# Encoder layer on one core: y stores of the late local blocks behind the next place's matmul, the last strip's 272-token block first, one y load of the third pass a tile sooner

## The chip, the cores and the metric

The kernel runs on one core of a Trainium2 chip. A core has five engines that each run their own list of instructions in order: PE (TensorE, matmuls), DVE (VectorE), ACT (ScalarE), POOL (GpSimd) and SP (SyncE, which here issues the transfers). An instruction waits on semaphores that other engines or transfers raise. The metric is the device time of one execution in microseconds, the median of three runs.

## The reference

One layer of an encoder is applied to two groups of tokens, a prompt of 1024 and a sample of 256, with the same 16 meta tokens put in front of each. Cut to what matters:

```python
def encoder_layer(h, ...):                       # h: (B, N, 2048), N = 16 + 1024 or 16 + 256
    u = rms_norm(h, norm_w) @ w_in               # 2048 x 6656: qa, ka, va, za, qb, kb, vb, zb
    qa, ka = rope(rms_norm(qa)), rope(rms_norm(ka))
    ya = global_gqa(qa, ka, va) * silu(za)       # 8 heads on 2 key heads, all keys
    qb, kb = rms_norm(qb), rms_norm(kb)
    yb = neighbourhood_attention(qb, kb, vb, rpb) * silu(zb)   # 8 heads, a window of 8 x 16 tokens and the meta keys
    return h + concatenate([ya, yb]) @ w_out     # 2048 x 2048
```

The outputs are the prompt's and the sample's tokens without the meta tokens, in float32. A head is 128 wide, so w_in is 52 strips of 128 columns.

## The kernel before

Every float32 product is three matmuls: the operands are split into a high part (cast on ACT, L62) and a low part (subtracted on DVE, L63), and hi·hi, hi·lo and lo·hi are added in PSUM.

**Projection.** Tokens are projected in two chunks. Chunk 1 has 512 tokens (sample, 240 of the prompt, meta). Chunk 2 has the other 784 of the prompt as two blocks of 512 and 272 (`BL`), whose split activations lie in the tiles "xa"/"x" and "xb". `strips` (L177 to L216) projects one strip: four chunks `c` of four k-tiles; in each chunk it loads w_in (`wr`, L194, from SP), splits it to `wh` and `wl`, and runs block by block four k-tiles of three matmuls (L211 to L213). The two blocks have a PSUM bank each (`pp`, four banks in all). After the second and the fourth chunk, `run_due` gives one "place" to attention work that is due.

**Evacuation.** A q strip goes through `qk_evac`: square on ACT (`ms`, L226), sum over partitions on POOL (`m`, L228), reciprocal square root on ACT and DVE (`rs_l`, `rs_r`, L72 to L74), product with the bank (L245), and a store to DRAM (`q2d`, L248). A z strip goes through `z_evac`: `z` (L267) reads the bank, four ACT functions, `za` (L272), `zt` (L275), and a store (`zd`, L785). Both go over the 512 block and then the 272 block. `z` of L267 is the last reader of a z strip's bank.

**Attention.** Global heads run between strips at some 750 to 1300 us. Then 24 late strips give 48 places, in which local heads 0 to 6 run: `scores` (L447, L280, L281 on PE) in one place, `values` (a y block of 256 tokens, L323 to L328) two places later. A y block is stored to `yd` (L328, from SP) as soon as it is there. The last strip of all is head 7's z. Head 7's keys and query are loaded back by `load_kq`: `qfull` (L801, L802) reads `q2d`, ACT (L62) and DVE (L63) split it to `q`. Head 7 runs in the first pass of the output projection.

**Output projection.** `outproj` makes seven passes (1, 2, 5, 6, 7, 3, 4) over five token tiles and two column halves; one step is 24 matmuls into a bank `pq` (L969 to L971). The `pq` pool takes over the four banks of `pp`. Its weights `ww` (L946 or L944) are loaded into the slots that xb leaves and split to `wm` in the slots of xa; the y operands are `yl`/`yh` in passes 1 and 2 (L910) and sums of two 512 KB loads `yr` (L904, `ysum` L930) from the third pass on.

**Order.** The Python code is traced, and a scheduler sets each engine's list when the kernel is built. It keeps the dependencies, goes by priority else, and `issue_after(x)` holds what is traced inside behind `x`. From the second pass on the lists keep the order of the code (`in_order`). A tile of a pool with one buffer can be written again only when its last reader, a transfer too, is done.

Of the kernel before, what the change touches and what calls it, by code (L numbers as in the profile page):

```python
# [12 lines left out]
F32 = mybir.dt.float32  # L13
# [7 lines left out]
P = 128  # L21
# [3 lines left out]
M3 = 3 * NMETA  # L25
# [14 lines left out]
QB = 256  # L40
# [8 lines left out]
NT = TH // P  # L49
# [6 lines left out]
class Kern:  # L56
# [120 lines left out]
    def strips(self, jobs, getx):  # L177


        nc, tc = self.nc, self.tc  # L180
        out = [[pool.tile([P, 512], F32, tag=tag, name="pp") for pool, tag in pools] for _, _, pools in jobs]
        for c in range(KT // WCH):
            ws = []
            for s, _, _ in jobs:
                with tc.high_priority(offset=self.woff):
                    w = self.raw.tile([P, WCH, P], F32, tag="raw", name="wr")
                    single = self.projected == 2 and c == 0 and not self.second
                    for i in range(0, WCH, 1 if single else WCH):
                        e = i + (1 if single else WCH)
                        self.lastw = nc.sync.dma_start(w[:, i:e], self.io["w_in"][s][:, c * WCH + i:c * WCH + e, :]).ins  # L190
                    wh = self.w.tile([P, WCH, P], F32R, tag="wh", name="wh")
                    wl = self.w.tile([P, WCH, P], F32R, tag="wl", name="wl")
                    if self.second and s not in AGAIN:
                        nc.sync.dma_start(wl[:].bitcast(F32), self.wld[s][:, c * WCH:(c + 1) * WCH, :])  # L194
                        nc.scalar.copy(wh[:], w[:])
                    else:
                        for i in range(0, WCH, 1 if single else WCH):
                            e = i + (1 if single else WCH)
                            self.lastsplit = self.split(wh[:, i:e], wl[:, i:e], w[:, i:e])
                            self.lasthi = self.hi  # L200
                ws.append((wh, wl))
                if not self.second and s not in AGAIN:
                    nc.sync.dma_start(self.wld[s][:, c * WCH:(c + 1) * WCH, :], wl[:].bitcast(F32))
            for b in range(len(jobs[0][1])):
                for k in range(WCH):
                    kt = c * WCH + k
                    xh, xl = getx(kt)[b]
                    first, last = kt == 0, kt == KT - 1
                    for (wh, wl), ps, (_, blocks, _) in zip(ws, out, jobs):
                        p, n = ps[b], blocks[b][1]  # L210
                        nc.tensor.matmul(p[:, :n], wh[:, k, :], xh[:, :n], start=first, stop=False)  # L211
                        nc.tensor.matmul(p[:, :n], wh[:, k, :], xl[:, :n], start=False, stop=False)  # L212
                        self.lastmm = nc.tensor.matmul(p[:, :n], wl[:, k, :], xh[:, :n], start=False, stop=last).ins  # L213
            if c % 2:
                self.run_due()
        return out  # L216

    def run_due(self):
        for _, f, a in next(self.due, ()):
            with self.tc.issue_after(self.lastmm):  # L220
                f(*a)
# [55 lines left out]
    def meta_scores(self, pm, meta, qh, ql, scale):  # L277

        nc = self.nc
        nc.tensor.matmul(pm[:ML + M3], meta, qh, start=True, stop=False)  # L280
        nc.tensor.matmul(pm[:ML + M3], meta, ql, start=False, stop=True)  # L281
        sm, sl = (self.sm.tile([M3, QB], F32, tag=n, name=n) for n in ("Sm", "Sl"))
        nc.scalar.activation(sl[:], pm[ML:ML + M3], AF.Copy, scale=scale)
        nc.vector.scalar_tensor_tensor(out=sm[:], in0=pm[:M3], scalar=scale, in1=sl[:], op0=ALU.mult, op1=ALU.add)
        return sm
# [27 lines left out]
    def put_y(self, po, tot, zs, ydst):  # L313

        nc = self.nc
        r = self.t.tile([P, QB], F32, tag="t", name="r")
        nc.scalar.activation(r[:], tot[:], AF.Ln)
        nc.scalar.activation(r[:], r[:], AF.Exp, scale=-1.0)
        nc.vector.tensor_tensor(out=tot[:], in0=tot[:], in1=r[:], op=ALU.mult)
        nc.vector.scalar_tensor_tensor(out=r[:], in0=tot[:], scalar=2.0, in1=r[:], op0=ALU.subtract, op1=ALU.mult)  # L320
        y = self.y.tile([P, QB], F32, tag="y", name="y")
        if len(zs.shape) == 3:
            nc.vector.tensor_tensor(out=y[:].rearrange("p (g r) -> p g r", g=4), in0=po[:].rearrange("p (g r) -> p g r", g=4),  # L323
                                    in1=zs, op=ALU.mult)
        else:
            nc.vector.tensor_tensor(out=y[:], in0=po[:], in1=zs, op=ALU.mult)
        nc.vector.scalar_tensor_tensor(out=y[:], in0=y[:], scalar=-1.0, in1=r[:], op0=ALU.mult, op1=ALU.mult)
        nc.sync.dma_start(ydst, y[:].rearrange("p (g r) -> p g r", g=ydst.shape[1]))  # L328

    def attend(self, q, zs, keys, meta, vals, vmeta, ydst):  # L330

# [243 lines left out]

    def chunk1(self):
        nc, io = self.nc, self.io
        self.due = iter(())
        self.woff, self.second, self.projected, self.sums = 0, False, 0, self.w_sums()
        self.scale2 = [self.one2.tile([P, T2], F32, tag=n, name=n) for n in ("rb2", "eb2")]  # L580
        self.xsq = {}
# [91 lines left out]
        for g in range(2):  # L673
# [4 lines left out]
            else:  # L678
                k, = pr(k_strip(KA + g, g, kw, True))
                (v, vm), = pr(v_strip(VA + g, g))  # L680
            for h in range(4 * g, 4 * g + 4):
                z, = pr(z_strip(ZA + h, h))
                q, = pr(q_strip(QA + h, h, qw, True))
                run(h, q, z, k, v, vm, None)
        for h in range(8):
            kj, qj = kb_strip(KB + h, 2 + h, kwb), qb_strip(QB_ + h, 8 + h, qwb)
            k, = pr(kj)
            q, = pr(qj)
            vj, zj = v_strip(VB + h, 2 + h), z_strip(ZB + h, 8 + h)
            if h < 7:  # L690
                (v, vm), = pr(vj)
                z, = pr(zj)
# [5 lines left out]
    def chunk2(self):  # L698
        nc, io = self.nc, self.io
# [26 lines left out]
        def v_rows_of(s, g):  # L726

            def evac(ps):
                for p, (o, n) in zip(ps, BL):
                    self.rows_out(self.v_rows(p, o, n), n, self.vn[g], C1P + o)  # L730
            return s, BL, evac
# [104 lines left out]

        def values(h, b):
            next(blocks.pop((h, b)), None)

        def local_heads():  # L840
            places = [[] for _ in range(LATE)]
# [18 lines left out]
        late = []  # L860
# [4 lines left out]
        def fill(n):  # L865
            for _ in range(min(n, len(late))):
                pr(late.pop(0))

        for g in range(2):
            if g == 0:  # L870
                k, _ = pr(k_strip(KA, 0, kw, True), v_rows_of(VA, 0))
            else:
                k, = pr(k_strip(KA + g, g, kw, True))
                pr(v_rows_of(VA + g, g))
            v = v_tiles(g)
            for h in range(4 * g, 4 * g + 4):
                z, = pr(z_strip(ZA + h, h) + (((self.sp, "sp"),) if h == 0 else ()))
                q, = pr(q_strip(QA + h, h, qw, True))
# [3 lines left out]
        load_kq(0)  # L882
        load_vz(0)
        self.due = iter(local_heads())
        fill(len(late))
        load_vz(NH - 1)
        self.due = iter([[(0, f, (NH - 1, b)) for f, b in ((values, n - 2), (scores, n)) if 0 <= b < 4] for n in range(6)])

# [119 lines left out]
    def outproj(self, end_attention):  # L1008
# [40 lines left out]
        for n in range(N):  # L1049
            p, t, b = step(n)  # L1050
            q, m = n // (2 * NT), n // 2
            if n == 2 * NT:
                end_attention()
                traced = len(self.nc.cur_bb.bb.instructions)
            if n - 2 in out:
                self.store(out.pop(n - 2), *step(n - 2))
            last = t == NT - 1
            if NT - 3 <= t < NT - 1:
                with self.tc.issue_after(self.lasty):
                    for j in range(4):  # L1060
                        load_w(q + 1, 8 * (t - NT + 3) + 4 * b + j)
            if q:
                for i in (n, n + 1, n + 2):
                    if i < N and i not in x:
                        x[i] = self.x_load(*step(i))
            direct = m + 1 < 2 * NT
            if direct:
                (load_y, make_y)[b](m + 1)
            elif m + 2 < M:
                load_y(m + 2)  # L1070
            if b == 0 and not direct:
                make_y(m + 1)
            ps = self.products([ws[q, 8 * b + k] for k in range(8)], ys[m])
            if last:
                for k in range(8):
                    make_w(q + 1, 8 * b + k)
            o = self.out_sums(p, 2 * t + b, ps, x.pop(n, None))
            if o:
                out[n] = o
            self.run_due()  # L1080
            if traced:
                traced = self.in_order(traced)
# [3 lines left out]
    def build(self):  # L1086
        tc, nc, io = self.tc, self.nc, self.io
        self.woff = 300
        nc.scalar.preload_act_table_set("natural_log_exp_and_others")
        with tc.tile_pool(name="dr", bufs=1, space=DRAM) as dp, tc.tile_pool(name="const", bufs=1) as cp, \  # L1090
# [19 lines left out]
            with ExitStack() as ps, ExitStack() as es_y:  # L1110
# [10 lines left out]
                pool(es_pp, "pp", 4, space=PSUM)  # L1121
                pool(ps, "mt", 1)
                self.meta_tiles()
                work = (("s", 5), ("ph", 2), ("sm", 2), ("mx", 2), ("t", 6))
                raw = self.raw
                with ExitStack() as es_1:
                    pool(es_1, "x", 16, side="right")
# [4 lines left out]
                pool(es_x, "x", 16, side="right", **kw)  # L1132
                pool(es_x, "xb", 16, side="right", **kw)
                pool(es_proj, "ev", 8, side="right", **kw)
                for name, bufs in (("k", 1), ("v", 1), ("tab", 1), ("q", 1), ("z", 1), *work, ("y", 1), ("qf", 1)):
                    pool(es_attn, name, bufs, **kw)
                self.chunk2()
                es_proj.close()
# [104 lines left out]
```

## Time and profile before

| what | us |
| --- | --- |
| three runs: median, lowest, highest | 2176.82, 2176.52, 2177.61 |
| profiled execution, its own time | 2173.82 |
| its span | 2172.0 |
| PE busy | 2154.0 (99%) |
| DVE, ACT, POOL busy | 1648.2 (76%), 1113.5 (51%), 523.4 (24%) |

The profile is one execution with start and duration of each instruction. A row of the list of waits has the waiting engine, tile and line, the releaser after the arrow, and then the time in us, the times and the longest. In a row of the timeline stand the start, the duration, engine, line, operation, tile written and tiles read, the shape and the count; a number in brackets is the wait ahead of it, with its releaser. A transfer's row shows the time on the issuing engine, and the landing has rows of its own. "PEclk" is the granted clock of TensorE as a share of full speed.

### The profile page before, as it was taken

The page shows a single profiled execution, that of the slowest core. Times are in us where ns is not written, and L with a number is a line of the kernel's source. Part 1 is how long each engine was busy: PE and PEld are TensorE (multiplying, and loading weights), DVE is VectorE, ACT ScalarE, POOL GpSimd, SP SyncE. Part 2 cuts the span into 40 slices and gives each one's busy share as a digit, 9 for nine tenths or more (in the row PEclk, how much of TensorE's full clock was granted, in tenths as well). Part 3 has the DMA queues.
Part 4 walks back from the last instruction along what each step waited for, and adds up shares of the span by engine and source line. Part 5 has one row for each costly group of instructions (what it writes and reads, how often), then busy time and mean ns, then how long its engine had stood idle before and what let it go on. Part 6 is the DMA issues. An engine that isn't in the chain of part 4 may idle for free.

```text
span 2172.0 us, 34106 instructions
## 1 busy us (share of the span) xinstructions
PE 2154.0 (99%) x11736; PEld 1879.0 (87%) x11736; DVE 1648.2 (76%) x2991; ACT 1113.5 (51%) x2294; POOL 523.4 (24%) x249
## 2 busy tenths in 40 slices
PE   9999999999999999999999999999999999999999
PEld 7888888888888999999999999989898988888887
DVE  8687976787864899997789988688777777455763
ACT  7556544555554666665666666444443464232230
POOL 1232422222311233231143224333333222000000
PEclk9999999999999999999999999999999999999999
DMA  8767889988554333334233344654433364663663
GB/s 301 222 198 230 281 285 322 348 276 264 176 187 145 103 110 106 116 115 139 98 115 98 109 131 143 188 160 139 135 124 121 125 202 133 219 241 102 232 224 107
DMA packets 263614, 383.83 MB, mean 177 GB/s; under 512 B 45040, under 2 KB 113296, under 8 KB 263440
## 3 DMA queue, kind: packets, MB, share of 16 engines
q1 hardware_dynamic: 263440, 381.65, 53.6%
q8 instruction: 92, 1.51, 0.3%
q14 instruction: 82, 0.67, 0.1%
HBM read 281.01 MB, written 100.38 MB: 176 GB/s over the span
## 4 chain that ended last, share of the span: by engine, by line
PE 90%; DVE 3%; DMA 3%; ACT 1%; issue 1%; SPq 1%; POOL 1%; DVEq 0%; ACTq 0%; POOLq 0%
PE pp L211 20%; PE pp L212 20%; PE pp L213 20%; PE pq L971 5%; PE pq L969 5%; PE pq L970 5%; PE sp L447 2%; PE po L481 1%; PE sp L343 1%; PE sp L342 1%; PE sp L341 1%; PE po L381 1%; PE po L382 1%; PE po L383 1%; PE tp L502 0%
## 5 line engine op out<-in xcount | busy, mean ns | idle before, releaser
L211 PE MATMUL pp<-x,wh 128*128 128x512 f32 (+1 forms) x1664 | 656.7, 396 | 5.4 <-ACT wh L62 5.3
L213 PE MATMUL pp<-x,wl 128*128 128x512 f32 (+1 forms) x1664 | 649.1, 390 | 0.0
L212 PE MATMUL pp<-x,wh 128*128 128x512 f32 (+1 forms) x1664 | 648.4, 390 | 0.0
L213 PEld LDWEIGHTS pp<-x,wl 128*128 128x128 f32 x1664 | 313.1, 188 | 62.3 <-DVE wl L63 0.9
L211 PEld LDWEIGHTS pp<-x,wh 128*128 128x128 f32 x1664 | 313.3, 188 | 61.8 <-ACT wh L62 6.3
L212 PEld LDWEIGHTS pp<-x,wh 128*128 128x128 f32 x1664 | 313.5, 188 | 52.6
L228 POOL PARTITION_ALL_REDUCE m<-ms x78 | 232.5, 2981 | 365.1 <-ACT ms L226 303.4
L63 DVE TENSOR_TENSOR wl<-wr,wh 128x512 fp32r<-128x512 f32 (+1 forms) x290 | 213.8, 740 | 126.0 <-ACT wh L62 103.2
L62 ACT CAST wh<-wr 128x512 fp32r<-128x512 f32 (+1 forms) x290 | 174.3, 606 | 216.8 <-PE pp L212 196.4
L310 POOL PARTITION_ALL_REDUCE tot<-a x80 | 177.1, 2214 | 445.2 <-DVE a L307 430.2
L212 PE MATMUL pp<-xb,wh 128*128 128x272 f32 x832 | 240.1, 289 | 0.0
L211 PE MATMUL pp<-xb,wh 128*128 128x272 f32 x832 | 239.6, 288 | 0.0
L213 PE MATMUL pp<-xb,wl 128*128 128x272 f32 x832 | 239.1, 287 | 0.0
L969 PE MATMUL pq<-wm,yh 128*128 128x512 f32 x560 | 219.2, 391 | 4.1 <-DVE z L267 3.1
L971 PE MATMUL pq<-wm,yl 128*128 128x512 f32 x560 | 218.9, 391 | 0.0
L970 PE MATMUL pq<-wm,yh 128*128 128x512 f32 x560 | 218.4, 390 | 0.0
L292 POOL PARTITION_ALL_REDUCE ma<-m x80 | 106.8, 1335 | 446.3 <-DVE m L290 441.7
L211 PEld LDWEIGHTS pp<-xb,wh 128*128 128x128 f32 x832 | 156.5, 188 | 7.3
L212 PEld LDWEIGHTS pp<-xb,wh 128*128 128x128 f32 x832 | 156.4, 188 | 7.1
L213 PEld LDWEIGHTS pp<-xb,wl 128*128 128x128 f32 x832 | 157.4, 189 | 0.1
L969 PEld LDWEIGHTS pq<-wm,yh 128*128 128x128 f32 x560 | 105.5, 188 | 26.4 <-ACT wm L62 3.2
L971 PEld LDWEIGHTS pq<-wm,yl 128*128 128x128 f32 x560 | 105.4, 188 | 22.3 <-DVE yl L63 0.4
(207 smaller groups left out, 3844.2 us busy)
## 6 DMA issues: line engine op xcount, KB each, us to landing
wr<-in_w_in SPq DMA_DIRECT2D x414, 256.0 KB, 3.4
wld<-wl SPq DMA_DIRECT2D x132, 256.0 KB, 4.3
wl<-wld SPq DMA_DIRECT2D x132, 256.0 KB, 3.1
yr<-yd SPq DMA_DIRECT2D x35, 512.0 KB, 5.2
wq<-in_w_out SPq DMA_DIRECT2D x64, 256.0 KB, 5.3
td<-wq SPq DMA_DIRECT2D x64, 256.0 KB, 4.3
ww<-td SPq DMA_DIRECT2D x64, 256.0 KB, 5.5
ww<-in_w_out SPq DMA_DIRECT2D x48, 256.0 KB, 5.1
```

Source lines behind the costliest of these rows:

```text
L62: self.hi = nc.scalar.copy(hi, full).ins
L63: return nc.vector.tensor_tensor(out=lo, in0=full, in1=hi.bitcast(F32), op=ALU.subtract).ins
L211: nc.tensor.matmul(p[:, :n], wh[:, k, :], xh[:, :n], start=first, stop=False)
L212: nc.tensor.matmul(p[:, :n], wh[:, k, :], xl[:, :n], start=False, stop=False)
L213: self.lastmm = nc.tensor.matmul(p[:, :n], wl[:, k, :], xh[:, :n], start=False, stop=last).ins
L228: nc.gpsimd.partition_all_reduce(m2[:], ms[:], P, RED.add)
L292: nc.gpsimd.partition_all_reduce(ma[:], m1[:], P, RED.max)
L310: nc.gpsimd.partition_all_reduce(tot[:], a1[:], P, RED.add)
L447: nc.tensor.matmul(dst, k[:, o:o + P], qfv[:, a:e, :], start=True, stop=True)
L969: nc.tensor.matmul(ps[:], yh, wh, start=k == 0, stop=False)
L970: nc.tensor.matmul(ps[:], yh, wl, start=False, stop=False)
L971: self.lastmm = nc.tensor.matmul(ps[:], yl, wh, start=False, stop=k == 7).ins
```

## The change

Four things, in the order of the diff:

1. In the last strip of all (`turn`), each chunk of four k-tiles runs the 272 block first and then the 512 block.
2. The y store of a late local block (`values`) is made to wait for the last projection matmul of the next place; `y` gets two buffers.
3. `Sl` of the meta scores comes from the ring `t`, which has seven buffers rather than six.
4. In the output projection, `load_y(10)`, the first y of the third pass, is traced a step sooner.

```diff
-            for b in range(len(jobs[0][1])):
+            nb = len(jobs[0][1])
+            for b in range(nb)[::-1] if self.turn else range(nb):
                 for k in range(WCH):
...
     def run_due(self):
+        if self.late:
+            self.tc.add_manual_dep(self.late.pop(0), self.lastmm.name, mybir.DependencyInfo(
+                mybir.DependencyClass.Sync, mybir.DependencyReason.DATA), reason="late store")
         for _, f, a in next(self.due, ()):
...
-        sm, sl = (self.sm.tile([M3, QB], F32, tag=n, name=n) for n in ("Sm", "Sl"))
+        sm = self.sm.tile([M3, QB], F32, tag="Sm", name="Sm")
+        sl = self.t.tile([P, QB], F32, tag="t", name="Sl")[:M3]
...
-        nc.sync.dma_start(ydst, y[:].rearrange("p (g r) -> p g r", g=ydst.shape[1]))
+        self.ystore = nc.sync.dma_start(ydst, y[:].rearrange("p (g r) -> p g r", g=ydst.shape[1])).ins
...
         def values(h, b):
             next(blocks.pop((h, b)), None)
+            self.late.append(self.ystore)
...
-        fill(len(late))
+        fill(len(late) - 1)
+        self.turn = True
+        fill(1)
...
                 (load_y, make_y)[b](m + 1)
+                if m + 2 == 2 * NT:
+                    load_y(m + 2)
...
-                work = (("s", 5), ("ph", 2), ("sm", 2), ("mx", 2), ("t", 6))
+                work = (("s", 5), ("ph", 2), ("sm", 2), ("mx", 2), ("t", 7))
...
-                for name, bufs in (("k", 1), ("v", 1), ("tab", 1), ("q", 1), ("z", 1), *work, ("y", 1), ("qf", 1)):
+                for name, bufs in (("k", 1), ("v", 1), ("tab", 1), ("q", 1), ("z", 1), *work, ("y", 2), ("qf", 1)):
```

The count of instructions is the same on every engine. Lines of the changed kernel are numbered 1 to 10 higher (L249 is L245 of before, L271 is L267, L918 is L910).

On PE, at the step from the last strip to the output projection, before has:

```order
L211 MATMUL pp<-xb,wh 128x272
L212 MATMUL pp<-xb,wh 128x272
L213 MATMUL pp<-xb,wl 128x272
L969 MATMUL pq<-wm,yh 128x512
L970 MATMUL pq<-wm,yh 128x512
```

In the same place PE has after:

```order
L212 MATMUL pp<-x,wh 128x512
L213 MATMUL pp<-x,wh 128x512
L214 MATMUL pp<-x,wl 128x512
L977 MATMUL pq<-wm,yh 128x512
L978 MATMUL pq<-wm,yh 128x512
```

The blocks have changed places, and so have their banks: the first `pq` writes the bank that held the last strip's 512 block before, and the one that held its 272 block after. The semaphore that this matmul waits for is raised by `z` of 128x512 in before, and by `z` of 128x272 in after.

On DVE, in the same place (`wm` are splits of w_out, `rs_r_20103` belongs to the 272 block of head 7's q), before has:

```order
L245 SCALAR_TENSOR_TENSOR rs_r_20103<-pp,nqkw,rs_r_20103 128x272
L63 TENSOR_TENSOR wm<-ww,wm 128x512 x3
L267 TENSOR_TENSOR z<-pp,rb_317 128x512
L63 TENSOR_TENSOR wm<-ww,wm 128x512 x3
L63 TENSOR_TENSOR yl<-yl,yh 128x512
L63 TENSOR_TENSOR wm<-ww,wm 128x512 x2
L272 SCALAR_TENSOR_TENSOR za<-z,za 128x512
L63 TENSOR_TENSOR wm<-ww,wm 128x512
L63 TENSOR_TENSOR yl<-yl,yh 128x512
L275 TENSOR_TENSOR zt<-z,za 128x512
L267 TENSOR_TENSOR z<-pp,rb_317 128x272
L63 TENSOR_TENSOR q<-qfull,q 128x1024
```

DVE has there after:

```order
L249 SCALAR_TENSOR_TENSOR rs_r_20103<-pp,nqkw,rs_r_20103 128x272
L63 TENSOR_TENSOR wm<-ww,wm 128x512
L271 TENSOR_TENSOR z<-pp,rb_317 128x512
L63 TENSOR_TENSOR wm<-ww,wm 128x512 x3
L63 TENSOR_TENSOR yl<-yl,yh 128x512 x2
L276 SCALAR_TENSOR_TENSOR za<-z,za 128x512
L63 TENSOR_TENSOR q<-qfull,q 128x1024
L279 TENSOR_TENSOR zt<-z,za 128x512
L271 TENSOR_TENSOR z<-pp,rb_317 128x272
```

The split of `q` now stands ahead of `zt` and of the 272 block's `z`, and more of the `wm` stand ahead of L249: from L73 of the 512 block of head 7's q to that row there are 11 `wm` now, and 7 before; a twelfth has gone from behind L73 to ahead of it.

On SP, before has there:

```order
L328 DMA yd_166<-y 128x4x64
L946 DMA ww<-in_w_out 128x512 x3
L910 DMA yl<-yd_165 128x512
L946 DMA ww<-in_w_out 128x512 x3
L248 DMA q2d_164<-rs_r_20089 128x512
L910 DMA yl<-yd_165 128x512
L946 DMA ww<-in_w_out 128x512 x7
L910 DMA yl<-yd_165 128x512
L946 DMA ww<-in_w_out 128x512 x3
L248 DMA q2d_164<-rs_r_20103 128x272
L910 DMA yl<-yd_165 128x512
L802 DMA qfull<-q2d_164 128x784
```

SP has there after:

```order
L954 DMA ww<-in_w_out 128x512 x4
L918 DMA yl<-yd_165 128x512
L954 DMA ww<-in_w_out 128x512 x7
L333 DMA yd_166<-y 128x4x64
L918 DMA yl<-yd_165 128x512
L954 DMA ww<-in_w_out 128x512
L252 DMA q2d_164<-rs_r_20089 128x512
L954 DMA ww<-in_w_out 128x512 x4
L918 DMA yl<-yd_165 128x512 x2
L252 DMA q2d_164<-rs_r_20103 128x272
L807 DMA qfull<-q2d_164 128x784
```

The y store has gone behind eleven of the `ww` loads, and the fourth `yl` load ahead of the 272 block's `q2d` store.

At the step from the second pass to the third (`yr`), SP has in before:

```order
L910 DMA yl<-yd_166 128x512 x2
L1006 DMA out_y<-o 128x512
L944 DMA ww<-td_235 128x512 x4
L960 DMA o<-in_xr 128x512
L1006 DMA out_y<-o 128x512
L904 DMA yr<-yd_165 128x1024
L904 DMA yr<-yd_166 128x1024
```

SP has at that step after:

```order
L918 DMA yl<-yd_166 128x512 x2
L912 DMA yr<-yd_165 128x1024
L912 DMA yr<-yd_166 128x1024
L1014 DMA out_y<-o 128x512
L952 DMA ww<-td_235 128x512 x4
L968 DMA o<-in_xr 128x512
L1014 DMA out_y<-o 128x512
```

The two loads of the third pass's first y have gone ahead of two stores of outputs, four weight loads and a load of x.

More of the change, by code (lines that the diff above doesn't have):

```diff
@@ L577, in chunk1 @@
         nc, io = self.nc, self.io
-        self.due = iter(())
+        self.due, self.late, self.turn = iter(()), [], False
         self.woff, self.second, self.projected, self.sums = 0, False, 0, self.w_sums()
```

## The prediction

> **What bounds the kernel now.** First I read the page's head and its chain, for the engine that carries the time.
>
> ```profile
> span 2172.0 us, 34106 instructions
> PE 90%; DVE 3%; DMA 3%; ACT 1%; issue 1%; SPq 1%; POOL 1%; DVEq 0%; ACTq 0%; POOLq 0%
> ```
>
> PE carries nine tenths of the chain, so an edit is worth what it adds to or takes from PE's idle time. Next came the list of PE's waits over the span, then the same list for 610 to 1770 us, where the late places lie (its only row is the fourth), and SP's waits.
>
> ```profile
> PE pp L211 <- ACT wh L62: 5.3, 1, 5.3
> PE pq L969 <- DVE z L267: 3.1, 1, 3.1
> PE pq L969 <- ACT yh L62: 1.0, 1, 1.0
> PE sm_ps L280 <- DVE mx L351: 1.1, 2, 0.5
> ...
> SPq L194 <- PE pp L213: 291.7, 94, 7.0
> SPq L328 <- DVE y L327: 84.4, 42, 5.2
> ```
>
> From 610 to 1770 us PE idles 1.1 us in all. SP is held by y stores for 84.4 us, and PE pays nothing for it. What can be won stands in two other rows, 3.1 at the first out-projection tile and 1.0 at a y operand. I looked at the first of them instruction by instruction.
>
> ```profile
> 1770.03 0.28 PE L213 MATMUL pp<-xb,wl 128*128 128x272 f32 x1
> 1772.54 0.69 DVE L267 TENSOR_TENSOR z<-pp,rb 128x512 f32<-128x512 f32 x1
> 1773.37 0.77 PE L969 MATMUL pq<-wm,yh 128*128 128x512 f32 x1 [3.06 <-DVE z L267]
> 1778.80 0.68 DVE L275 TENSOR_TENSOR zt<-z,za 128x512 f32<-128x512 f32 x1
> 1779.40 0.43 DVE L267 TENSOR_TENSOR z<-pp,rb 128x272 f32<-128x272 f32 x1
> 1780.09 1.22 DVE L63 TENSOR_TENSOR q<-qfull,q 128x1024 fp32r<-128x1024 f32 x1 [0.26 <-ACT q L62]
> 1780.34 0.60 PE L447 MATMUL sp<-qfull,kfull 128*128 128x128 f32 x4
> 1780.70 0.36 PE L280 MATMUL sp<-q,km 128*112 128x256 f32 x1
> 1781.37 0.37 PE L281 MATMUL sp<-q,km 128*112 128x256 f32 x1 [0.31 <-DVE q L63]
> 1782.09 0.53 PE L969 MATMUL pq<-wm,yh 128*128 128x512 f32 x1
> 1787.71 0.61 PE L447 MATMUL sp<-qfull,kfull 128*128 128x128 f32 x4
> 1788.07 0.36 PE L280 MATMUL sp<-q,km 128*112 128x256 f32 x1
> 1788.27 0.28 PE L281 MATMUL sp<-q,km 128*112 128x256 f32 x1
> ```
>
> The last strip ends at 1770.31. The first `pq` waits until 1773.37, since its bank is the last strip's 512 block, which DVE reads out only at 1772.54, behind splits of w_out. DVE reads the 272 block at 1779.40, and nothing waits for that.
>
> **The turn.** It exchanges the banks: `pq` now waits for the 272 block's `z`. PE's work in the strip is the same, but it finishes the 272 block 2.8 us before the strip's end (twelve matmuls of 128x512 follow, half of the 5.62 that 24 take from 1782.09 to 1787.71), and that helps only if DVE comes to it sooner. It doesn't: the `z` of 128x272 is still behind the 512 block's, and now also behind the split of `q`. That split needs `qfull` back from DRAM, which needs the `q2d` store, which needs L245 on the 272 block of head 7's q (L249 in after). So PE stands at the end of a chain of two transfers that before lay beside the first `pq` tile's matmuls. Its links:
>
> ```profile
> 1759.00 0.62 ACT L72 ACTIVATE rs_l<-rs_r 128x512 f32<-128x512 f32 x1
> 1759.66 1.25 DVE L73 TENSOR_TENSOR rs_l<-m,rs_l 128x512 f32<-128x512 f32 x1 [2.17 <-ACT rs_l L72]
> 1762.15 0.74 DVE L245 SCALAR_TENSOR_TENSOR rs_r<-pp,nqkw,rs_r 128x512 f32<-128x512 f32 x1
> 1770.32 0.50 DVE L245 SCALAR_TENSOR_TENSOR rs_r<-pp,nqkw,rs_r 128x272 f32<-128x272 f32 x1
> ...
> L229 DVE TENSOR_TENSOR m<-m,eb 128x272 f32<-128x272 f32 x1 | 0.4, 435 | 0.0
> ...
> 1771.00 4.99 DMA q2d<-rs_r
> 1776.00 2.98 DMA qfull<-q2d
> 1779.01 1.06 ACT q L62
> 1780.09 1.23 DVE q L63
> ...
> DMA to landing us min/median/max: 1.8/3.1/6.9
> ```
>
> The last row is the view of the tile `q2d` from 1300 to 1790 us: the store and the reload over all such heads.
>
> Step one, when L245 on 272 runs. In after, twelve `wm`, two `yl`, L73 and L74 of the 512 block stand ahead of it from 1759.65 on, the time at which ACT's first cast ends if it stands where L72 stood (1759.00 + 0.62). An operation of 0.68 is followed 0.60 later (1778.80 to 1779.40), so these 16 take 9.6. L245 on 512 takes 0.74 less that overlap of 0.08, 0.66, and L229, L73 and L74 on 272 take 0.435 less 0.08 each, 1.07. In before one of the 0.69 operations took 1.25 (at 1759.66, beside POOL's sum): 0.56 more. The sum is 11.89, so L245 starts at 1771.54 and ends at 1772.04, against 1770.82 before. I take DVE as busy throughout, since the `ww` loads that it splits go out some 3 us sooner: in before SP stood at the y store until then.
>
> ```profile
> 1756.91 0.36 SPq L328 DMA_DIRECT2D yd<-y  x1
> 1757.33 1.46 SPq L946 DMA_DIRECT2D ww<-in_w_out  x3
> ```
>
> Step two, the transfers. The `q2d` store took 4.99 in before, with loads of w_out queued ahead of it; the view's minimum is 1.8. In after those loads are out sooner and should mostly have landed, so I take 2.4, between the minimum and the median of 3.1. From 1772.04 it is 0.05 to the issue, 2.4 to the landing (1774.49), 2.98 for `qfull` (1777.47), 1.06 on ACT (1778.53), 1.23 for the split on DVE (1779.76), 0.60 for `zt`, 0.43 for the 272 block's `z` (1780.79), and 0.14 to the matmul (1772.54 + 0.69 to 1773.37). `pq` starts at 1780.93 instead of 1773.37: **+7.6**. With 1.8 for the store and without the 0.56 it is +6.4; with 4.99 it is +10.2.
>
> The fourth `yl` load ahead of the store on SP waits for the last strip's last matmul, which frees its slot; that ends at about 1770.3 in either kernel, so it hides behind DVE.
>
> Step three, the clock. `pq` began on a slow clock:
>
> ```profile
> core 0: us, PE busy (x) PEld busy (x) DVE busy (x) ACT busy (x) POOL busy (x), PEclk, DMA share, GB/s
> 1770.30:1773.40 3.10, 0.04 (x2) 0.06 (x1) 3.10 (x7) 2.82 (x5) 0.00 (x0) 0.92 1.03 379
> 1773.40:1776.30 2.90, 2.90 (x7) 2.35 (x8) 2.75 (x5) 2.90 (x7) 0.00 (x0) 0.50 0.81 307
> ```
>
> The first tile took 6.97 (1773.37 to 1780.34), the second 5.62 (1782.09 to 1787.71): 1.35 is already paid for an idle time of 3.06. The longer idle time gets no further price in the sum; for the upper end I allow a second such stretch, half of 2.90, 1.45. The Trainium skill (TensorE: Matmul & The Clock Gate, Part 1: The HAM clock gate) says that the clock is halved after about one idle window of 3.4 us and comes back after one busy window, whose phase runs freely. By that rule a longer idle time costs at most a window at half speed, an estimate of 1.7 in place of 1.35, and the sum would be 0.35 higher; the trace's 0.50 agrees on the half, and its 2.90 is shorter than a window.
>
> Step four, what comes back. In before the scores between the first two `pq` tiles waited for `q` (L280 to L281 is 0.67, and 0.20 the next time, 1788.07 to 1788.27). In after `q` is ready before the first `pq` starts: **-0.5**.
>
> **The third pass's y.** Its two loads were issued with two more, and the operand came late:
>
> ```profile
> 1889.20 1.23 DVE L930 TENSOR_TENSOR ysum<-yr 128x1024 f32<-128x1024 f32 x1 [4.58 <-DMA yr<-yd]
> 1905.26 0.39 PE L971 MATMUL pq<-wm,yl 128*128 128x512 f32 x1
> 1906.67 0.50 PE L969 MATMUL pq<-wm,yh 128*128 128x512 f32 x1 [1.02 <-ACT yh L62]
> 1907.39 0.50 PE L971 MATMUL pq<-wm,yl 128*128 128x512 f32 x1
> ```
>
> DVE stood 4.58 for the landing, and the splits behind it came late at 1906.67, where a matmul started 1.41 after the one before rather than 0.23 (5.62 over 24). With the loads ahead of four weight loads and two stores, the 4.58 shrinks by more than PE lost, 1.18 there and 0.26 over the next two (0.72 against 0.46): **-1.4**, or nothing if the weights' splits are what is late then.
>
> **Stores, buffers, `Sl`.** A late y store now waits for one more matmul. Behind it on SP stand weight loads, which wait for matmuls as it is (the 291.7 us at L194), and PE idles 1.1 in that stretch: 0. The second `y` buffer takes away the wait of the next y for the store; without it the later store would hold DVE. `Sl` moves to another ring with one buffer more: 0. All of it also shifts the scheduler's order in the global heads, where some attention matmuls come earlier on PE than their producers do; the 1.1 us of idle time shows that there is nothing to gain there, and at two groups of up to 3 us I allow 0 to +6 and take 0.
>
> **Sum.** 7.6 - 0.5 - 1.4 = +5.7. The profiled execution would go from 2173.82 to 2179.5, its span from 2172.0 to 2177.7. It is 3.0 below the median of the runs, so the median goes from 2176.82 to 2182.5.
>
> **Rivals.**
> - *The turn takes no more than the 512 block's `z`* (not slower). If `pq`'s wait ends with `z` of 128x512, it starts where it did, at 1773.4, as DVE reads that block at about the same place of its list; the 0.5 and the 1.4 are won: 2174.9, within 0.2%. For it speaks the row of before that names this releaser. Against it speaks the semaphore in the built program. It decides if the row of the first `pq` is released by the 512 block's.
> - *The turn does what its words promise*: the 272 block is read during the strip's last chunk, the 3.06 and the clock's 1.35 go, too: 2176.8 - 3.06 - 1.35 - 1.9 = 2170.5. DVE's list speaks against it.
> - *The chain is longer*: the store lands after 4.99 as before and the clock is slow for a second stretch: 10.2 + 1.45 - 1.9 = +9.75, 2186.6. The transfers' share of 1.03 up to 1773.40 speaks for it, the sooner loads against it.
> - *New waits in the global heads or behind late stores*: another +6, 2188.5. Against it speaks that SP is held for 84.4 us by y stores without a cost.
>
> **How the numbers follow.** A difference of 0.2%, 4.4 us, is about what a measurement of this kernel can tell from none. The forecast gets 0.78, with its own range from 2181.3 (+6.4 and both gains) to 2187.0 (+10.2, and no gain); a twentieth of them lose less than 4.4, by a shorter landing. The 512 block's `z` gets 0.07, the promised gain 0.04, the longer chain 0.05, the new waits 0.06. So faster is 0.04, the same 0.07 and 0.04 of the forecast's, 0.11, and slower 0.85. The range leaves out the two cases that gain and the far end of the new waits: 2179.0 to 2188.5.
>
> **What would show it.** The first `pq` starts near 1781, held about 10 us by `z` of L271 on 128x272, with two transfers, ACT's and DVE's `q` just ahead in the chain; the granted clock is 0.5 for some 3 us behind it; L280 to L281 takes 0.2; the wait for `yh` at the third pass is gone; PE's idle time from 610 to 1770 us stays at about 1 us. The forecast is wrong if DVE reaches the 272 block without the split of `q` ahead, if the transfers land in under 1.5 us each, or if PE's idle time grows elsewhere.

## The result and the profile after

Over 20 runs of each kernel on the same chip the changed one has a median of 2180.18 us (2178.63 to 2184.09), the one before 2176.51 us (2173.01 to 2181.15). The medians lie 3.7 us apart. The ratio over all the runs is 1.0021, with a 95% interval of 1.0014 to 1.0027: slower by 3.0 to 5.9 us. The forecast was 2182.5, from 2179.0 to 2188.5.

The profiled executions lie further apart than the medians. That of after took 2184.09, the longest of its 20; that of before, 2173.82, is among the shorter ones. So spans are not compared below, but what happens in a stretch. These are the first five rows of the list of PE's waits in the profile of after (the rest are of 0.6 us and less):

```profile
PE pq L977 <- DVE z L271: 10.9, 1, 10.9
PE pp L212 <- ACT wh L62: 6.9, 2, 5.5
PE po L386 <- ACT ph L62: 1.8, 2, 1.6
PE tp L265 <- DVE vm L63: 1.3, 1, 1.3
PE tp L265 <- DVE vt L258: 0.6, 1, 0.6
...
```

The first out-projection tile now waits 10.9 us instead of 3.1. The wait for `yh` at the third pass (1.0) and the two for `mx` in the global heads (1.1) are no longer there. The second row has one wait more than in before, of 1.4 us at 14 us. The kernel before with nothing but the sooner y load, shown below, has a second one in this row as well (7.5 in two), so it isn't put down to the change. The same list, for 1775 to 2180 us alone, has its first row and nothing else. The chain of waits from 1775 to 1785 us names each link (start, duration, what), down to the first `pq` matmul:

```profile
1775.33 0.48 DVE rs_r L249
1775.81 0.02 issue
1775.83 2.33 DMA q2d<-rs_r
1778.16 0.02 issue
1778.18 3.17 DMA qfull<-q2d
1781.35 0.02 issue
1781.37 1.05 ACT q L62
1782.42 0.02 issue
1782.45 1.23 DVE q L63
1783.67 0.60 DVE zt L279
1784.27 0.36 DVE z L271
1784.63 0.14 issue
1784.77 0.77 PE pq L977
```

Read upwards, `pq` stands behind the 272 block's `z`, that behind `zt` and the split of `q`, that behind ACT's cast, the reload, the store, and the 272 block of head 7's q (L249). The timeline of DVE and PE shows where the stretch of DVE ahead of this chain begins, and what follows the wait:

```profile
1763.38 1.26 DVE L63 TENSOR_TENSOR wm<-ww,wm 128x512 fp32r<-128x512 f32 x1 [2.15 <-ACT wm L62]
1773.52 0.39 PE L214 MATMUL pp<-x,wl 128*128 128x512 f32 x1
1776.32 0.68 DVE L271 TENSOR_TENSOR z<-pp,rb 128x512 f32<-128x512 f32 x1
1784.77 0.77 PE L977 MATMUL pq<-wm,yh 128*128 128x512 f32 x1 [10.86 <-DVE z L271]
1792.82 0.60 PE L452 MATMUL sp<-qfull,kfull 128*128 128x128 f32 x4
1793.18 0.36 PE L284 MATMUL sp<-q,km 128*112 128x256 f32 x1
1793.38 0.28 PE L285 MATMUL sp<-q,km 128*112 128x256 f32 x1
1896.43 1.22 DVE L938 TENSOR_TENSOR ysum<-yr 128x1024 f32<-128x1024 f32 x1
```

The last strip ends at 1773.91 (1773.52 + 0.39). The 512 block's `z`, for which the first tile waited before, runs at 1776.32, 8.4 us before the tile starts. The third pass's `ysum` has no wait ahead of it, where it had 4.58. The clock behind the long wait (windows of the profile of after):

```profile
core 0: us, PE busy (x) PEld busy (x) DVE busy (x) ACT busy (x) POOL busy (x), PEclk, DMA share, GB/s
1784.80:1788.60 3.80, 3.80 (x9) 3.04 (x10) 0.89 (x2) 1.58 (x4) 0.00 (x0) 0.50 0.26 99
1788.60:1789.60 1.00, 1.00 (x3) 0.72 (x3) 0.00 (x0) 0.00 (x0) 0.00 (x0) 0.50 0.08 26
1789.60:1790.40 0.80, 0.80 (x4) 0.65 (x3) 0.00 (x0) 0.00 (x0) 0.00 (x0) 0.70 0.30 87
```

PE ran at half clock for about 5 us, not for 2.90. The first tile took 8.05 us (1784.77 to 1792.82), against 6.97 in before. From the last strip's end to the first matmul of the third pass, after takes 132.60 (1773.91 to 1906.51) and before 124.30 (1770.31 to 1894.61). This stretch is called the step to the out-projection below.

### The profile page after: what moved, and what is told of

It reads as the page before. It is cut to its first block, busy times and chain, and to the rows that moved or that the text cites. A ratio compares the mean times of both kernels' runs of the same rounds, so it can differ in the third digit from the quotient of the medians.

```text
span 2182.3 us, 34104 instructions
## 1 busy us (share of the span) xinstructions
PE 2155.9 (99%) x11736; PEld 1880.1 (86%) x11736; DVE 1648.3 (76%) x2991; ACT 1116.0 (51%) x2294; POOL 528.3 (24%) x249
## 4 chain that ended last, share of the span: by engine, by line
PE 93%; DMA 3%; DVE 2%; ACT 1%; SPq 1%; issue 1%; POOL 0%; DVEq 0%; ACTq 0%; POOLq 0%
PE pp L212 20%; PE pp L214 20%; PE pp L213 20%; PE pq L977 6%; PE pq L979 6%; PE pq L978 6%; PE sp L452 2%; PE po L486 2%; PE sp L347 1%; PE sp L346 1%; PE sp L348 1%; PE po L386 1%; PE po L387 1%; PE po L388 1%; PE tp L507 0%
## 5 line engine op out<-in xcount | busy, mean ns | idle before, releaser
L63 DVE TENSOR_TENSOR wl<-wr,wh 128x512 fp32r<-128x512 f32 (+1 forms) x290 | 219.3, 759 | 124.2 <-ACT wh L62 88.6
L232 POOL PARTITION_ALL_REDUCE m<-ms x78 | 224.7, 2881 | 355.3 <-ACT ms L230 299.6
L315 POOL PARTITION_ALL_REDUCE tot<-a x80 | 187.2, 2340 | 437.9 <-DVE a L312 415.8
L977 PE MATMUL pq<-wm,yh 128*128 128x512 f32 x560 | 219.6, 392 | 10.9 <-DVE z L271 10.9
L977 PEld LDWEIGHTS pq<-wm,yh 128*128 128x128 f32 x560 | 105.8, 189 | 33.1 <-issue 11.3
L978 PEld LDWEIGHTS pq<-wm,yh 128*128 128x128 f32 x560 | 105.8, 189 | 22.0
```

The source lines that it names most:

```text
L63: return nc.vector.tensor_tensor(out=lo, in0=full, in1=hi.bitcast(F32), op=ALU.subtract).ins
L232: nc.gpsimd.partition_all_reduce(m2[:], ms[:], P, RED.add)
L315: nc.gpsimd.partition_all_reduce(tot[:], a1[:], P, RED.add)
L977: nc.tensor.matmul(ps[:], yh, wh, start=k == 0, stop=False)
L978: nc.tensor.matmul(ps[:], yh, wl, start=False, stop=False)
```

## The experiments

The theory: the loss is the turn's, through the bank in which the first `pq` tile lands. The rivals: the loss lies in the late stores or the shifted order of the global heads; or the late chain holds the out-projection's weights and y as well, whatever the bank. Each median stands beside one of the kernel before that was measured with it, and the rows come from the profile of one execution.

### The change without the turn

```diff
-        fill(len(late) - 1)
-        self.turn = True
-        fill(1)
+        fill(len(late))
```

> All of the change but the turn of the last strip. Theory (the loss is the turn's: the first out-projection tile stands in the bank of the block whose readout is behind the reload and split of q): the first tile waits 3.1 us again, for z of 128x512; the third pass's wait for yh (1.4 with what follows) and the two waits of the meta scores for mx (1.4, gone in the profile of after) stay gone, so about 2.8 us under the kernel before, 2173.7 where that one has 2176.5. Rival (the loss lies in the late stores or in the shifted order of the global heads): it stays where the changed kernel is, 2179 to 2180.

Measured: 2175.24 against 2177.65, ratio 0.9992 (0.9983 to 1.0). The first tile's wait is 2.44 and names the 512 block's `z`:

```profile
1777.13 0.47 PE L975 MATMUL pq<-wm,yh 128*128 128x512 f32 x1 [2.44 <-DVE z L271]
1785.91 0.37 PE L285 MATMUL sp<-q,km 128*112 128x256 f32 x1 [0.91 <-DVE q L63]
```

Without the turn the loss is gone, so the late stores and the global heads' order don't carry it. The second row is new to the theory: `q` is late as well, by 0.91 here and 0.31 in before. The split of `q` ends 11.2 us after the last strip's end in this profile and 11.0 after it in before, so a first tile that is done sooner only waits longer for it.

### The turn alone

The edit is the loop over the blocks and the three lines of `fill` from the diff, put into the kernel before, and nothing else.

> The kernel before with the turn and nothing else of the change. Theory: the first out-projection tile waits 10 to 11 us for z of 128x272 instead of 3.1, L280 to L281 falls from 0.67 to 0.20, the waits for yh at the third pass and for mx stay: +7.3, 2183.8 where before has 2176.5. Rival: no change, 2176.5, and the first tile waits about 3.

Measured: 2185.09 against 2177.65, ratio 1.0039 (1.0026 to 1.0052), so +7.4 between the medians, where +7.3 was expected.

```profile
1790.04 0.76 PE L972 MATMUL pq<-wm,yh 128*128 128x512 f32 x1 [12.15 <-DVE z L268]
```

The turn alone makes the long wait, and the waits for `mx` and `yh` are there as in before. The wait is longer than the 10 to 11 expected: the 272 block's product (L246 here) starts 3.0 us after the last strip's end, and 1.4 after it in the changed kernel.

### The changed kernel with another bank for the first tile

```diff
+        for _ in range(2):
+            d = self.pq.tile([P, FB], F32, tag="pq", name="none")
+            self.nc.vector.memset(d[:, :1], 0.0)
         load_y(0)
```

The pool gives out its four banks in turn, so the first two tiles of the output projection now get the banks of the strip before the last.

> The changed kernel, turn and all, with two tiles of pq taken and written (one column each, on DVE) ahead of the first, so that the first two out-projection tiles get the banks of the strip before the last and the third and fourth those of the last strip. DVE's order is that of the changed kernel but for the two writes. Theory (the bank is the cause): the first tile no longer waits for z; what is late next is the split of q for the scores behind it, which in the profile of after ended 9.9 us after the last strip, against 5.5 for a tile: a new wait of some 4 us there. So 7 us under the changed kernel, 2173 to 2174 where that has 2180. Rival (something else in the changed order delays the out-projection, its weights or its y): the wait stays near 10 us under another name, 2180.

Measured: 2175.40 against 2177.65, ratio 0.9991 (0.9982 to 1.0). The turn and, but for the two writes, DVE's order are as in the changed kernel, and the loss is gone, 2.2 under before where the changed kernel is 3.7 above it:

```profile
1775.25 0.39 PE L977 MATMUL pq<-wm,yh 128*128 128x512 f32 x1
1782.84 0.68 PE L452 MATMUL sp<-qfull,kfull 128*128 128x128 f32 x4 [1.99 <-DMA qfull<-q2d]
1783.83 0.55 PE L284 MATMUL sp<-q,km 128*112 128x256 f32 x1 [0.30 <-ACT q L62]
1785.09 0.56 PE L285 MATMUL sp<-q,km 128*112 128x256 f32 x1 [0.71 <-DVE q L63]
```

The first tile starts with the strip's end (1775.25, with no wait). The scores behind it wait 3.0 us in three steps for the reload, the cast and the split of `q`. So the bank made the 10.9 us, and head 7's `q` is the next limit, about as the theory said (4 us were expected). The granted clock is 0.50 for 6.8 us from 1783.7 on, and the step to the out-projection takes 125.49: 7.1 less than in the changed kernel, but not less than the 124.30 of before. As far as one profile tells, the 2.2 under before come from the other parts of the change.

### The turn as its words have it

```diff
-                for p, (o, n) in zip(ps, BL):
+                for p, (o, n) in list(zip(ps, BL))[::-1] if self.turn else zip(ps, BL):
                     zt = self.ev.tile([P, n], F32, tag="ev", name="zt")
```

The last strip's 272 block is not only computed first but also read out first.

> The changed kernel with the last strip's readout turned too: z of 128x272 comes ahead of z of 128x512 in the trace, and so on DVE, where it stands behind L74 of the 272 block of head 7's q and ahead of L249. That is the turn doing what its words say. Theory (a chain through head 7's q, and not the first tile, is the limit there): the first tile waits 1 us or less, but the scores behind it wait 3 to 4 us for qfull and the split of q, as in e6_bank: 2175 to 2176 where before has 2177.6, no better than without the turn. Rival (the first tile's wait and the slow clock are the limit): 3.1 + 1.35 + 0.5 + 2.8 under before, 2170.

Measured: 2172.84 against 2177.27, ratio 0.9981 (0.9973 to 0.999), so 4.4 under before. Its PE timeline:

```profile
1772.02 0.47 PE L977 MATMUL pq<-wm,yh 128*128 128x512 f32 x1 [0.66 <-DVE z L271]
1778.52 0.68 PE L452 MATMUL sp<-qfull,kfull 128*128 128x128 f32 x4 [0.77 <-DMA qfull<-q2d]
1779.50 0.37 PE L284 MATMUL sp<-q,km 128*112 128x256 f32 x1 [0.30 <-ACT q L62]
1780.76 0.37 PE L285 MATMUL sp<-q,km 128*112 128x256 f32 x1 [0.89 <-DVE q L63]
```

The first tile waits 0.66, and 2.0 come back in front of the scores, less than expected. Behind them the clock is slow (0.50 from 1781.3 to 1784.7). In this profile the step to the out-projection takes 124.25, as much as in before (124.30): what the first tile wins is paid again at the scores. The time lies between the two theories, 2 to 3 us better than I said and 3 worse than the rival. That it beats the kernel without the turn isn't shown: the intervals of the two ratios overlap.

### The other parts alone

The third pass's `load_y` by itself, in the kernel before:

> The kernel before with the third pass's first y loaded a tile sooner, and nothing else. Theory: the wait for yh at the third pass goes, 1.2 to 1.4 us, and nothing else moves: 2176.2 where before has 2177.6. Rival (the weights' splits are late then): 0.

Measured: 2176.06 against 2177.27, ratio 0.9992 (0.9983 to 1.0); the wait for `yh` is gone from its list. The times don't tell 1.2 us from none, but the traces do: from the start of the third pass's first tile (1894.61 in before) to PE's end (2168.38) it is 273.77 in before, and 272.16 in this kernel, in the changed one, in the one without the turn and in the best one alike. That is 1.61.

The late stores, with two `y` buffers and `Sl` in the ring, in the kernel before:

> The kernel before with the late y stores, two y buffers and Sl in the ring of t, without the turn and the sooner y load. Theory: the stores cost and gain nothing; the meta scores' two waits for mx (1.4 us together) go, since Sl no longer has a ring of two; the first out-projection tile waits 2.5 to 3: 2176.2 where before has 2177.6. Rival (the sooner weight loads of the first pass, no longer held behind the last y store, shorten the first tile's wait): 2 us more, 2174.

Measured: 2177.11 against 2177.27, ratio 0.9998 (0.9989 to 1.0007). The interval runs from 2.4 us under before to 1.5 above it, so the time doesn't tell whether the 1.4 was won. The waits for `mx` are gone. The first tile waits 2.43 rather than 3.06, but the scores behind it now wait 1.8 for the cast and the split of `q`, which ends 10.9 us after the strip, as in before. `Sl` in the ring by itself, run once:

> The kernel before with Sl in the ring of t with seven buffers, and nothing else. Theory: this alone takes away PE's two waits for mx in the global heads (0.5 each, 1.4 with what follows), which are gone in every kernel that has it so far. Rival (the late stores do): the two waits are there.

Its one time is 2174.83, beside 2176.04 of before, and tells nothing at such a distance. Its list of PE's waits does; its first four rows are

```profile
PE pp L211 <- ACT wh L62: 5.4, 1, 5.4
PE pq L970 <- DVE z L267: 4.0, 1, 4.0
PE po L382 <- ACT ph L62: 1.5, 1, 1.5
PE pq L970 <- ACT yh L62: 1.4, 1, 1.4
```

and no row of `sm_ps`: the ring alone takes away the waits for `mx`, without the late stores.

### Towards a better kernel: the bank, and head 7's scores a step later

```diff
-        self.due = iter([[(0, f, (NH - 1, b)) for f, b in ((values, n - 2), (scores, n)) if 0 <= b < 4] for n in range(6)])
+        self.due = iter([[(0, f, (NH - 1, b)) for f, b in ((values, n - 3), (scores, n - 1)) if 0 <= b < 4] for n in range(7)])
```

This goes with the two written `pq` tiles, and without the turn.

> The changed kernel without the turn, with the two written pq tiles, and with head 7's scores and values one step later in the first pass (behind the second tile instead of the first). Theory: the first tile has no wait, q is there when the scores come, and the slow clock behind the wait goes, too: 2176.5 - 2.8 - 3.1 - 1.35 - 0.55 = 2168.7; up to 2 us more if the second tile's weights are split too late. Rival (the wait only moves: weights or y operands are as late as z): 2173.7, as without the turn.

Measured: 2174.57 against 2177.65, ratio 0.9988 (0.9979 to 0.9996): well under half of what was expected. Both waits are gone, and one took their place, at the second scores, behind the third tile (timeline of PE and DVE):

```profile
1791.07 0.69 DVE L63 TENSOR_TENSOR yl<-yl,yh 128x512 fp32r<-128x512 f32 x1 [6.69 <-ACT yh L62]
1792.30 0.87 DVE L457 SCALAR_TENSOR_TENSOR S<-sp,bt 128x256 f32<-128x256 f32 x2
1792.85 1.20 PE L452 MATMUL sp<-qfull,kfull 128*128 128x128 f32 x4 [3.21 <-DVE S L457]
```

DVE's list had the split of the third token tile's y ahead of the first scores' readout, and stood there 6.7 us for a load. So that split was put behind the readout (`lasts` is its last instruction on DVE, `lastsl` the one on ACT):

```diff
-                (load_y, make_y)[b](m + 1)
+                if 2 <= n <= 5 and b:
+                    with self.tc.issue_after(self.lasts), self.tc.issue_after(self.lastsl):
+                        make_y(m + 1)
+                else:
+                    (load_y, make_y)[b](m + 1)
```

> The kernel of e9_bank_later, in which the third scores' matmuls waited 3.2 us for DVE, which stood 6.7 us at the split of the third token tile's y ahead of the first scores' readout. Here that split (and its cast on ACT) is held behind the readouts of the scores. Theory: the 3.2 us go, and no other wait takes their place: 3 us under e9_bank_later, about 6 under the kernel before (2171 where that has 2177.6). Rival: the y operand is then what comes late at the fifth step, and the time stays at that of e9_bank_later.

Measured: 2168.97 against 2177.27, ratio 0.9958 (0.9945 to 0.997). The whole list of PE's waits of 0.2 us and more:

```profile
PE pp L212 <- ACT wh L62: 5.5, 1, 5.5
PE po L386 <- ACT ph L62: 1.6, 1, 1.6
PE tp L265 <- DVE vm L63: 1.4, 1, 1.4
PE po L389 <- DVE Pm L307: 0.3, 1, 0.3
```

Nothing at the step to the out-projection is left in it. This beats both kernels, by 8.3 and by about 12 us. In the profiles the step takes 119.03 instead of 124.30, so some 5 of the 8.3 were won there. Two more kernels take it apart. With the turn put back:

> The kernel of e11_hold_y with the turn of the last strip put back. Theory (the turn costs only through the bank that the first out-projection tile takes): with another bank for that tile and the scores a step later it costs nothing, 2169 where before has 2177.3, and no wait at the first tile. Rival (the turn costs something of its own, by its order of splits and loads): 2 us or more above e11_hold_y.

Measured: 2168.30 against 2176.04, ratio 0.9967 (0.9954 to 0.9979), no loss against the one without the turn within the intervals. The turn costs nothing of its own that can be seen. Without the two written tiles (and without the turn):

> The kernel of e11_hold_y without the two written pq tiles, so that the first out-projection tile is in the bank of the last strip's 512 block again. Theory: its wait for z of 128x512 is back, 2.4 to 3.1 us, and a slow clock behind it, 1.35 to 2.5 us: 4 to 5.5 above e11_hold_y, 2173 to 2174.5 where before has 2177.3. Rival (the later scores and the held split alone bring the gain): 2169.

Measured: 2172.51 against 2176.04, ratio 0.9985 (0.9976 to 0.9994). The wait is back:

```profile
1773.72 0.47 PE L975 MATMUL pq<-wm,yh 128*128 128x512 f32 x1 [2.52 <-DVE z L271]
```

Under before it is 3.5, and with the other bank 8.3: the bank is worth about 4.8 once the other two waits are gone: the wait of 2.52, and a slow clock behind it (the first tile took 7.16, to 1780.88, against 5.47 in the kernel with the other bank).

## Why the prediction was right, point by point

**The turn's mechanism** was right: the releaser, the chain and its order are those forecast. The terms by link, from L249's start to `pq`: forecast 9.39 (1771.54 to 1780.93), measured 9.46 (1775.31 to 1784.77); in it the store took 2.33 (2.4), the reload 3.17 (2.98), ACT 1.05 (1.06). The short store is the turn's: it took 2.14 with the turn alone, where the y stores had not moved, and 5.1 without the turn, where they had. The stretch of DVE ahead of L249, forecast 11.89, took 11.93 (1763.38 to 1775.31), with the stretched operation of 1.26 in it. The wait came to 10.86, where 10.6 follows from the forecast. That DVE was busy throughout, an assumption, held.

**The clock** was undersized in this execution. I took no further price for the longer idle time, and up to 1.45 more for the upper end; the tile paid 1.08 more than before's (8.05 against 6.97), inside that. But the idle time's length isn't the reason. In other profiles a wait of 3.35 (the kernel with `load_y` alone) had a first tile of 8.15, and one of 12.15 (the turn alone) of 7.45:

```profile
1778.60 0.76 PE L969 MATMUL pq<-wm,yh 128*128 128x512 f32 x1 [3.35 <-DVE z L267]
1786.75 0.49 PE L447 MATMUL sp<-qfull,kfull 128*128 128x128 f32 x3
...
1797.49 0.60 PE L448 MATMUL sp<-qfull,kfull 128*128 128x128 f32 x4
```

The last row is of the turn alone, whose tile starts at 1790.04, above. The granted clock, read in windows of 0.5 us, is 0.50 in stretches of 3.4 us (before, 1772.9 to 1776.3), 6.8 us (`load_y` alone, 1777.3 to 1784.1) and 13.7 us (after, 1776.4 to 1790.1; the turn alone, 1780.4 to 1794.0). These are one, two and four times the same length. A tile pays only for the part of a stretch in which PE has work, in after the last 5.3 of the 13.7. That fits a window whose phase runs freely, as the Trainium skill has it (TensorE: Matmul & The Clock Gate, Part 1: The HAM clock gate). The estimate from that page of at most one window, 1.7, doesn't hold: some 5 us at half clock cost 2.6, against the 5.47 that a first tile takes in the best kernel, where there is no wait (1770.26 to 1775.73).

**L280 to L281** is 0.20 in after (1793.18 to 1793.38): the -0.5 came.

**The third pass**: -1.4 forecast, -1.6 measured in the traces.

**The stores** cost and gained nothing that the time can tell, as forecast.

**`Sl`** was the step that failed, by its size: I read 1.1 us of idle time from 610 to 1770 us as "nothing to gain there" and wrote 0. The ring took away just that idle time, and with the spacing of the matmuls around the two places it comes to 1.4 (0.7 at each in before, none in after). How much of it reaches the time isn't settled: from the 2501st projection matmul (610.78 in before) to the last, the one profile of the ring alone has 1158.52 where before has 1159.25, 0.7 less. New waits in the global heads, the rival with +6, did not come. PE's idle time from 610 to 1770 us is 1.7 in after; 1.3 of that is a wait for `vm` at 611.5, which before has at 609.6, ahead of this stretch.

**The sum** of what the traces show is 7.8 for the wait (10.86 - 3.06), -0.5, -1.6, -0.7 to -1.4, and 0 to 1.1 for the clock: +4.3 to +6.1, where 3.0 to 5.9 were measured. The forecast's +5.7 lacked the 0.7 to 1.4.

**The size** was too high. The median of 2180.18 lies 2.3 below the forecast, and below the range that was worked out for the forecast itself, which begins at 2181.3; only the stated range, which reaches down to 2179.0, has it. The room below was left for a shorter landing of the store, and the landing came as forecast (2.33), so it was partly luck that the range was wide enough. 0.3 of the 2.3 is the base, a median of 2176.82 over three runs where twenty have 2176.51. A loss above 0.2% was given 0.85, and the measured interval, 0.14% to 0.27%, lies on both sides of that line.

**The rival that the turn does what it promises** was given too large a gain, with 2170.5. The kernel that does it is 4.4 under before and not 6.3, and in its profile none of that was won at the step to the out-projection (124.25 against 124.30). A limit stood right behind the wait removed: head 7's `q`, which ended within a microsecond of the first tile in before (L281's wait of 0.31), holds the scores for 2 to 3 us as soon as the tile is earlier, and the slow clock comes behind that wait instead. I had this row in the prediction, but counted it as a gain and not as a bound. **That the first tile waits for the 512 block's `z`** fell: the semaphore in the built program told which block it is.

## What to carry to other kernels

A reordering on one engine can hand a buffer to another user: look up who holds the bank or slot that the next stage takes first, and where its last reader stands in its engine's list; here two narrow writes that moved the rotation by two banks took the whole loss away, but gained next to nothing until the next limits were gone, too. Before pricing a wait that is to go, add up what is ready when: the next operand was 0.3 us behind. Removing three waits in a row (bank, `q`, y's split) shortened the step from 124.30 to 119.03, where the first alone, with the turn in, left it at 125.49. A wait of a microsecond in a stretch that seems clean is still a term of the sum.

## What the runs showed of the hardware that was not expected

The price of a slow clock after a wait did not follow the length of the wait. First tiles took 6.97, 8.15, 8.05 and 7.45 us after waits of 3.06, 3.35, 10.86 and 12.15, and 5.47 after none. After two waits of nearly the same length, 2.44 (without the turn) and 2.43 (late stores), they took 7.14 and 5.72; in the second of these the clock fell to 0.50 only a tile later, from 1783.1 to 1786.5, behind the waits for `q`. Here the stretches at half clock lasted 3.4, 6.8 or 13.7 us, in steps of one length, and they began as late as after PE was back at work: without the turn at 1777.9, where PE's wait had ended at 1777.13.
